# Attention heads in a two-layer trunk: order of the key tiles, place of the compressed branch, and which engine scales the probabilities

## The chip, the cores and the metric

The kernel runs on one core of a Trainium2 chip. The metric is device time in microseconds (us), the median of repeated executions; one further execution was taken with the hardware profiler, and its trace is what is read below. The core has five engines that run side by side and wait for each other by semaphores: TensorE (PE) for matmuls, VectorE (DVE), ScalarE (ACT) and GpSimd (POOL) for elementwise work, and SyncE (SP), which here issues DMAs. Matmuls write PSUM (eight banks of 128 x 512 f32); POOL works on SBUF tiles only in this kernel.

## What is computed

The reference is a decoder trunk of two layers on 512 tokens of width 1024. Each layer has one input projection, three mixers side by side (sparse attention with 8 heads, gated linear attention, spatial gating), an output projection, and a gated feed-forward part. The change lies in the attention mixer alone. Of its reference, cut to the parts that matter:

```python
p_cmp = masked_softmax(s, ...)                 # 31 compressed keys
o_cmp = einsum('bghqc,bcgd->bqghd', p_cmp, vc)
p = masked_softmax(s, tok <= t)                # selected blocks: with 512 tokens all of them
o_slc = einsum('bghqm,bgqmd->bqghd', p, vsel)
p = masked_softmax(s, wmask)                   # window of 512 tokens: all earlier ones
o_win = einsum('bghqk,bkgd->bqghd', p, vwb)
return gb[..., 0:1] * o_cmp + gb[..., 1:2] * o_slc + gb[..., 2:3] * o_win
```

So each head has two causal branches (br 0 selected, br 1 window) over 512 keys and one branch over 31 compressed keys, and its output is the gated sum of the three.

## The kernel before

The attention heads are computed one after the other in a Python loop over 8 heads (`hp`, `hh`) and two branches (`br`), written out into instructions; a scheduler of the framework then orders each engine's instructions ahead of time, so on each engine they run in one fixed order. Tokens are cut into four tiles of 128. For query tile i only the keys up to 128 (i + 1) matter, so its probabilities are a tile of 128 rows and 128, 256, 384 or 512 columns.

For one branch of one head the steps are:

- Scores. PE multiplies queries and keys into a PSUM bank (ring "s", three banks; lines L1217 and L1218 for tiles 0 and 1, both branches at once, L1236 and L1237 for tiles 2 and 3). DVE takes the row maxima (L1220, L1239), ACT the exponentials with their row sums (L1224, L1241).
- Scaling. DVE takes the reciprocals `rc` of the four row sums (L1246) and multiplies those of tiles 0 to 2 with the gate (`rr`, L1247). Then, in the order of `SORD`, DVE scales tiles 0 and 1 (L1255), ACT tile 2 (L1253) and POOL tile 3 (L1251), in place. POOL takes `rc` and the gate as two factors. A dependency written by hand lets POOL start only when DVE's second scaling is done.
- Turning. PE transposes the blocks of the scaled tiles into a PSUM bank (ring "t", two banks, L1264), in three groups `JG`: key tile 0 (4 blocks, 512 columns), key tile 1 (3 blocks, 384 columns), key tiles 2 and 3 (2 + 1 blocks, 384 columns).
- Eviction. Each group is cut into a high and a low part: ACT casts the bank to a tile PT (L301, inside the helper `split_psum`), DVE subtracts it from the bank (L302).
- Product. PE multiplies the values (`vst`) with the high and the low part (L1277, L1278) and adds up all of both branches in one PSUM bank, O (ring "o", one bank).

At the end of a head two more matmuls add the compressed branch (`pcT`, `vcb`; L1288, L1289), whose probabilities were made once per group of four heads. Then ACT copies one half of O (L1290), and DVE adds the other half to it (L1291), which frees O for the next head. After two heads the result is split in two parts by ACT (L301) and DVE (L302) for the output projection.

Matmuls of the output projection's other half (L338 to L340), for mixers that are already done, stand between the attention instructions on PE; their weights are cast by ACT (L320) and subtracted by DVE (L323). The query operands of later heads are copied by POOL (L1188).

Tiles are handed out from rings: the probabilities of tiles 0 and 1 have three buffers each and those of tiles 2 and 3 two (`P0B`), PT three.

## Time and profile before

| what | us |
|---|---|
| median of 3 runs | 1285.01 (1283.91 to 1285.46) |
| the profiled execution, its own time | 1285.18 |
| its span (first to last instruction) | 1283.4 |
| PE busy | 1257.9 (98%) |
| DVE busy | 916.0 (71%) |
| ACT busy | 676.1 (53%) |
| POOL busy | 152.9 (12%) |

The attention heads lie at about 180 to 280 us of the span (first layer) and 810 to 910 us (second layer). Busy time is the union of an engine's instructions as they are drawn; the ends of matmuls are modelled. A row of a group reads: line, engine, operation, output <- inputs, shapes, count | busy us, mean ns of one | idle us of the engine just before them, and what ended it. A row of the timeline reads: start, length, engine, line, operation, tiles, shapes, count, and in brackets the idle time before it and what ended it.

### The profile page before, as it was taken

Reading aid. Unit: us, or ns where it says so; the run is one execution under the profiler, and the core shown is the slowest. Engines: PE = TensorE matmul, PEld = TensorE weight load, DVE = VectorE, ACT = ScalarE, POOL = GpSimd, SP = SyncE. Lnnn points to the kernel's source line nnn. Section 1 sums busy time; section 2 is a strip of 40 time slices with the busy share of each in tenths; the row PEclk is TensorE's granted clock in tenths of the full one; section 3 lists DMA queues with packets and bytes.
Section 4 is the critical chain, followed back from the end, with each engine's and each line's share of the span. In section 5 each row is a group of like instructions: output and inputs, shape, how many; then the busy total and the mean of one; then the engine's idle time right before and its main releaser. Section 6 shows DMA issues by size and latency. Waiting matters only on the chain.

```text
span 1283.4 us, 18048 instructions
## 1 busy us (share of the span) xinstructions
PE 1257.9 (98%) x6678; PEld 1039.6 (81%) x6678; DVE 916.0 (71%) x1645; ACT 676.1 (53%) x1288; POOL 152.9 (12%) x157
## 2 busy tenths in 40 slices
PE   8999999999999999999999999999999999999997
PEld 7887788778888888888888887877788888888886
DVE  6667799977855775577546669998767457827775
ACT  5676357864533553354446743788544345515532
POOL 0101121112000100010301003111210001000102
PEclk9999999999999999999999999999999999999999
DMA  6461341034335885483335316210533448744811
GB/s 231 125 197 34 104 120 33 17 85 129 99 101 141 193 238 148 101 198 111 105 103 148 118 34 169 70 33 3 147 99 98 132 118 220 212 123 134 227 66 66
DMA packets 134203, 155.01 MB, mean 121 GB/s; under 512 B 9306, under 2 KB 86884, under 8 KB 134116
## 3 DMA queue, kind: packets, MB, share of 16 engines
q1 hardware_dynamic: 117392, 128.81, 33.1%
q0 software_dynamic: 10208, 20.84, 9.1%
q10 hardware_dynamic: 6516, 4.22, 1.4%
q8 instruction: 52, 0.85, 0.3%
q14 instruction: 35, 0.29, 0.1%
HBM read 149.92 MB, written 2.10 MB: 118 GB/s over the span
## 4 chain that ended last, share of the span: by engine, by line
PE 80%; DVE 10%; ACT 5%; DMA 2%; issue 2%; ACTq 0%; POOL 0%; DVEq 0%; POOLq 0%
PE banks L338 22%; PE banks L339 22%; PE banks L340 22%; PE banks L1264 2%; DVE PT L302 2%; PE banks L1277 1%; PE banks L1278 1%; DMA raw<-in_w_in_dram 1%; ACT hl L320 1%; PE banks L1601 1%; DVE nmx L1239 1%; PE banks L473 1%; DVE hl L323 1%; PE banks L971 1%; DVE w1h L745 1%
## 5 line engine op out<-in xcount | busy, mean ns | idle before, releaser
L320 ACT CAST hl<-raw 128x1024 fp32r<-128x1024 f32 (+3 forms) x170 | 175.2, 1034 | 226.0 <-PE banks L340 177.5
L323 DVE TENSOR_TENSOR hl<-raw,hl 128x1024 fp32r<-128x1024 f32 (+3 forms) x170 | 206.5, 1219 | 93.2 <-ACT hl L320 90.9
L338 PE MATMUL banks<-hl,kt 128*128 128x512 f32 (+2 forms) x688 | 258.0, 375 | 1.0 <-ACT hl L320 1.0
L339 PE MATMUL banks<-hl,kt 128*128 128x512 f32 (+2 forms) x688 | 256.4, 373 | 0.2 <-DVE hl L323 0.2
L340 PE MATMUL banks<-hl,kt 128*128 128x512 f32 (+2 forms) x688 | 256.2, 373 | 0.0
L339 PE MATMUL banks<-kt,hl 128*128 128x512 f32 x384 | 151.5, 394 | 0.1
L340 PE MATMUL banks<-kt,hl 128*128 128x512 f32 x384 | 151.1, 393 | 0.0
L338 PE MATMUL banks<-kt,hl 128*128 128x512 f32 x384 | 150.5, 394 | 0.0
L338 PEld LDWEIGHTS banks<-hl,kt 128*128 128x128 f32 x688 | 129.4, 188 | 23.4 <-ACT hl L320 1.8
L339 PEld LDWEIGHTS banks<-hl,kt 128*128 128x128 f32 x688 | 129.5, 188 | 22.0 <-DVE hl L323 0.6
L340 PEld LDWEIGHTS banks<-hl,kt 128*128 128x128 f32 x688 | 129.4, 188 | 21.9
L320 ACT CAST hl<-wx 128x1024 fp32r<-128x1024 f32 x48 | 50.5, 1052 | 79.8 <-PE banks L340 66.7
L339 PEld LDWEIGHTS banks<-kt,hl 128*128 128x128 f32 x384 | 72.2, 188 | 14.8 <-DVE kt L297 0.9
L340 PEld LDWEIGHTS banks<-kt,hl 128*128 128x128 f32 x384 | 72.1, 188 | 13.8
L338 PEld LDWEIGHTS banks<-kt,hl 128*128 128x128 f32 x384 | 72.0, 188 | 13.2 <-ACT kt L301 0.3
L323 DVE TENSOR_TENSOR hl<-wx,hl 128x1024 fp32r<-128x1024 f32 x48 | 58.7, 1223 | 19.0 <-ACT hl L320 18.8
L502 DVE TENSOR_TENSOR xT<-xT,banks 128x512 f32<-128x512 f32 x56 | 37.5, 680 | 48.0 <-PE banks L340 48.0
L339 PE MATMUL banks<-act,hl 128*128 128x512 f32 x172 | 67.0, 390 | 0.0
L340 PE MATMUL banks<-act,hl 128*128 128x512 f32 x172 | 66.9, 389 | 0.0
L338 PE MATMUL banks<-act,hl 128*128 128x512 f32 x172 | 66.9, 390 | 0.0
L302 DVE TENSOR_TENSOR PT<-banks,PT 128x384 fp32r<-128x384 f32 (+1 forms) x96 | 54.6, 597 | 13.3 <-ACT PT L301 12.4
L339 PE MATMUL banks<-hl,act 128*128 128x512 f32 (+1 forms) x164 | 63.0, 384 | 0.0
(356 smaller groups left out, 2394.5 us busy)
## 6 DMA issues: line engine op xcount, KB each, us to landing
raw<-in_w_gate_dram SPq DMA_DIRECT2D x44, 512.0 KB, 3.8
raw<-in_w_up_dram SPq DMA_DIRECT2D x44, 512.0 KB, 4.0
raw<-in_w_in_dram SPq DMA_DIRECT2D x32, 512.0 KB, 3.7
raw<-in_w_down_dram SPq DMA_DIRECT2D x36, 256.0 KB, 3.6
raw<-in_w_down_dram SPq DMA_DIRECT2D x18, 512.0 KB, 4.0
raw<-in_w_out_dram SPq DMA_DIRECT2D x16, 512.0 KB, 4.3
raw<-in_cmp_w_k_dram SPq DMA_DIRECT2D x8, 512.0 KB, 3.8
raw<-in_cmp_w_v_dram SPq DMA_DIRECT2D x8, 512.0 KB, 4.6
```

The source lines that it names most:

```text
L302: nc.vector.tensor_tensor(lo, src, hi.bitcast(F32), op=ALU.subtract)
L320: last_cast[:] = [nc.scalar.copy(hl[:, 0, 0:n], raw[:, 0:n])]
L323: e_.tensor_tensor(hl[:, 1, 0:n], raw[:, 0:n], hl[:, 0, 0:n].bitcast(F32), op=ALU.subtract)
L338: nc.tensor.matmul(ps, lh, rh, start=start, stop=False, skip_group_check=skip)
L339: nc.tensor.matmul(ps, lh, rl, start=False, stop=False, skip_group_check=skip)
L340: return nc.tensor.matmul(ps, ll, rh, start=False, stop=stop, skip_group_check=skip)
L473: ins = nc.tensor.matmul(pw[t], xkt[n][:, kk, p, t * P : t * P + P], eu[n][0][:, q, kk, :], start=n == 0 and p + q + kk == 0, stop=n == 3 ...
L502: nc.vector.tensor_tensor(xT[:, m, :], xT[:, m, :], ps, op=ALU.add)
L745: nc.vector.tensor_tensor(hl[:, 1], raw[:, q * 512 : q * 512 + 512], hl[:, 0].bitcast(F32), op=ALU.subtract)
L971: nc.tensor.matmul(banks[:, 2 + h, lv * 64 : lv * 64 + 64], Es[t][r, lv, :], xqs[t][r, lv, :], start=True, stop=True)
L1239: nc.vector.tensor_reduce(nmx, S[:, 0:n], axis=AX.X, op=ALU.max, negate=True)
L1264: nc.tensor.transpose(T[:, c : c + P], ps_[i][:, j * P : (j + 1) * P], ident)
```

## The change

Five things change in the attention heads:

- DVE no longer scales. POOL scales tile 3, then 1, then 0 (512, 256, 128 columns), each with `rc` and the gate as two factors; ACT still scales tile 2. The dependency between POOL and DVE is gone with DVE's scalings.
- `rr` is one column (tile 2) and not three.
- The order of scaling is 3, 2, 1, 0.
- The groups are turned and multiplied in the order key tiles (2, 3), then 1, then 0, in all branches but the first of head 0.
- In heads 1 to 7 the two matmuls of the compressed branch open the sum in O, and the product of key tile 0 of the second branch closes it. Head 0 is summed as before.

```diff
@@ -43,7 +43,7 @@
 WPOOL = {}
 WSITE = {}
 XKP = ()
-SORD = (0, 1, 2, 3)
+SORD = (3, 2, 1, 0)
 TT = "tttt"
 ATAGS = "gggggggg"
 OT = "o"
@@ -51,7 +51,7 @@
 PREP = {(0, 0): (("q", 0), ("q", 1)), (0, 1): (("c", 0),), (0, 3): (("d", 0),), (1, 0): (("q", 2),), (2, 0): (("q", 3),), (2, 3): (("c", 1),),
         (4, 0): (("d", 1),)}
 NBOTH = 2
-ISP = (3,)
+ISP = (3, 1, 0)
 ISA = (2,)
 PBK = {"g": 2, "s": 3, "t": 2, "o": 1}
 JG = ((0,), (1,), (2, 3))
@@ -1242,21 +1242,16 @@
                                 ps_.append(p_)
                             if br == 0:
                                 prep(h, 1)
-                            rc, rr = small(NT, "rc", 4), small(NT, "rr", 4)
+                            rc, rr = small(NT, "rc", 4), small(1, "rr", 4)
                             nc.vector.reciprocal(rc, den)
-                            nc.vector.tensor_tensor(rr[:, 0:3], rc[:, 0:3], gates[:, 0:3, 3 * h + 1 + br], op=ALU.mult)
-                            scaled = None
+                            nc.vector.tensor_tensor(rr, rc[:, 2:3], gates[:, 2:3, 3 * h + 1 + br], op=ALU.mult)
                             for i in SORD:
                                 if i in ISP:
-                                    p3 = nc.gpsimd.tensor_scalar(ps_[i], ps_[i], rc[:, i : i + 1], gates[:, i, 3 * h + 1 + br : 3 * h + 2 + br], op0=ALU.mult, op1=ALU.mult)
-                                elif i in ISA:
-                                    nc.scalar.activation(ps_[i], ps_[i], AF.Copy, scale=rr[:, i : i + 1])
+                                    nc.gpsimd.tensor_scalar(ps_[i], ps_[i], rc[:, i : i + 1], gates[:, i, 3 * h + 1 + br : 3 * h + 2 + br], op0=ALU.mult, op1=ALU.mult)
                                 else:
-                                    scaled = nc.vector.tensor_scalar(ps_[i], ps_[i], rr[:, i : i + 1], None, op0=ALU.mult)
-
-                            tc.add_manual_dep(p3.ins, scaled.ins.name, mybir.DependencyInfo(mybir.DependencyClass.Sync, mybir.DependencyReason.DATA),
-                                              reason="port")
-                            for js in JG:
+                                    nc.scalar.activation(ps_[i], ps_[i], AF.Copy, scale=rr)
+                            lhc = vcb[:, g, h4].rearrange("p s d -> p (s d)")
+                            for js in (JG if h == 0 and br == 0 else JG[::-1]):
                                 T = psum(TT[js[0]])
                                 c = 0
                                 for j in js:
@@ -1269,24 +1264,28 @@
                                 else:
                                     pf = mp.tile([P, c], F32, tag="PT", name=nm("PT"), bufs=3)
                                     nc.scalar.copy(pf, T[:, 0:c])
+                                if first and h > 0:
+                                    nc.tensor.matmul(O, lhc, pcT[g][0], start=True, stop=False)
+                                    nc.tensor.matmul(O, lhc, pcT[g][1], start=False, stop=False)
+                                    first = False
                                 c = 0
                                 for j in js:
                                     n = SEQ - j * P
                                     lhs = vst[:, j, br, g].rearrange("p s d -> p (s d)")
                                     if js[0] < JS:
                                         nc.tensor.matmul(O[:, j * P : SEQ], lhs, pt[:, 0, c : c + n], start=first, stop=False)
-                                        nc.tensor.matmul(O[:, j * P : SEQ], lhs, pt[:, 1, c : c + n], start=False, stop=False)
+                                        nc.tensor.matmul(O[:, j * P : SEQ], lhs, pt[:, 1, c : c + n], start=False, stop=h > 0 and br == 1 and j == 0)
                                     else:
                                         nc.tensor.matmul(O[:, j * P : SEQ], lhs.bitcast(F32), pf[:, c : c + n],
                                                          start=False, stop=False)
                                     first = False
                                     c += n
                         prep(h, 3)
-                        lhs = vcb[:, g, h4].rearrange("p s d -> p (s d)")
                         hs = slice(64 * hh, 64 * hh + 64)
                         ls = slice(64 - 64 * hh, 128 - 64 * hh)
-                        nc.tensor.matmul(O, lhs, pcT[g][0], start=False, stop=False)
-                        nc.tensor.matmul(O, lhs, pcT[g][1], start=False, stop=True)
+                        if h == 0:
+                            nc.tensor.matmul(O, lhc, pcT[g][0], start=False, stop=False)
+                            nc.tensor.matmul(O, lhc, pcT[g][1], start=False, stop=True)
                         nc.scalar.copy(oc[hs, :], O[ls, :])
                         nc.vector.tensor_tensor(oc[hs, :], oc[hs, :], O[hs, :], op=ALU.add)
                     split_psum(kt[:, hp % 2, 0, :], kt[:, hp % 2, 1, :], oc)
```

Line numbers behind the change are 5 lower at L1264 (L1259 after) and 1 lower at L1277 to L1291; POOL's scaling, L1251 before, is L1250.

How the instructions now stand is shown at three places around head 6 of the first layer. On PE, the first place is the step from head 5 to head 6. Before, the second matmul of head 5's compressed branch comes first, then the turns of head 6's first branch (`ident,P`), two score matmuls, and the first product of head 6:

```order
L1289 MATMUL banks<-pcT_2402,vcb_279 128x512
L1264 MATMUL banks<-ident,P_2649 128x128
L1264 MATMUL banks<-ident,P_2657 128x128
L1264 MATMUL banks<-ident,P_2665 128x128
L1264 MATMUL banks<-ident,P_2671 128x128
L1264 MATMUL banks<-ident,P_2657 128x128
L1264 MATMUL banks<-ident,P_2665 128x128
L1264 MATMUL banks<-ident,P_2671 128x128
L1236 MATMUL banks<-km_181_1599,qst_1807 128x384
L1237 MATMUL banks<-km_183_1601,qm_187_1605 128x384
L1277 MATMUL banks<-PT_2685,vst_277 128x512
```

In the changed kernel the same place on PE, from head 5's last product to head 6's first compressed matmul:

```order
L1277 MATMUL banks<-PT_2632,vst_277 128x512
L1259 MATMUL banks<-ident,P_2657 128x128
L1259 MATMUL banks<-ident,P_2665 128x128
L1259 MATMUL banks<-ident,P_2671 128x128
L1218 MATMUL banks<-km_183_1601,qm_187_1605 128x512
L1259 MATMUL banks<-ident,P_2649 128x128
L1259 MATMUL banks<-ident,P_2657 128x128
L1259 MATMUL banks<-ident,P_2665 128x128
L1259 MATMUL banks<-ident,P_2671 128x128
L1236 MATMUL banks<-km_181_1599,qst_1807 128x384
L1237 MATMUL banks<-km_183_1601,qm_187_1605 128x384
L1268 MATMUL banks<-pcT_2401,vcb_279 128x512
```

Between the last matmul of one head and the first of the next stand seven turns and two score matmuls before, and seven turns and three score matmuls now.

On DVE, the second place is the first branch of head 6, from its reciprocal on (`den` are the row sums, P_2649 and P_2657 tiles 0 and 1). Before:

```order
L1246 RECIPROCAL rc_2673<-den_2643 128x4
L1247 TENSOR_TENSOR rr_2674<-rc_2673,gates_280 128x3
L1239 TENSOR_REDUCE nmx_2716<-banks 128x1
L302 TENSOR_TENSOR PT_2620<-banks,PT_2620 128x384
L302 TENSOR_TENSOR PT_2628<-banks,PT_2628 128x384
L1255 TENSOR_SCALAR P_2649<-P_2649,rr_2674 128x128
L1255 TENSOR_SCALAR P_2657<-P_2657,rr_2674 128x256
```

In the changed kernel, DVE from the same reciprocal on, with the next branch's reciprocal (rc_2722), to the sum that frees O:

```order
L1246 RECIPROCAL rc_2673<-den_2643 128x4
L1220 TENSOR_REDUCE nmx_2763<-banks 128x2
L1247 TENSOR_TENSOR rr_2674<-rc_2673,gates_280 128x1
L302 TENSOR_TENSOR PT_2632<-banks,PT_2632 128x512
L302 TENSOR_TENSOR PT_2684<-banks,PT_2684 128x384
L1246 RECIPROCAL rc_2722<-den_2644 128x4
L1220 TENSOR_REDUCE nmx_2771<-banks 128x2
L1290 TENSOR_TENSOR tmp_2396<-tmp_2396,banks 64x512
```

The scalings are gone, and one row maximum now stands between the reciprocal and its product with the gate, which ACT's tile waits for.

On POOL, the third place is the queue of scalings around head 6. Before, from head 5's first branch to head 7's first:

```order
L1251 TENSOR_SCALAR P_2551<-P_2551,rc_2553,gates_280 128x512
L1251 TENSOR_SCALAR P_2598<-P_2598,rc_2600,gates_280 128x512
L1251 TENSOR_SCALAR P_2671<-P_2671,rc_2673,gates_280 128x512
L1251 TENSOR_SCALAR P_2718<-P_2718,rc_2720,gates_280 128x512
L1251 TENSOR_SCALAR P_2787<-P_2787,rc_2789,gates_280 128x512
```

In the changed kernel POOL's queue for head 5's second branch and head 6's first:

```order
L1250 TENSOR_SCALAR P_2600<-P_2600,rc_2602,gates_280 128x512
L1250 TENSOR_SCALAR P_2539<-P_2539,rc_2602,gates_280 128x256
L1250 TENSOR_SCALAR P_2531<-P_2531,rc_2602,gates_280 128x128
L1250 TENSOR_SCALAR P_2671<-P_2671,rc_2673,gates_280 128x512
L1250 TENSOR_SCALAR P_2657<-P_2657,rc_2673,gates_280 128x256
L1250 TENSOR_SCALAR P_2649<-P_2649,rc_2673,gates_280 128x128
```

Each branch has one scaling on POOL before and three now, the widest first.

## The prediction

> **What bounds the kernel now.** I read the page first.
>
> ```profile
> span 1283.4 us, 18048 instructions
> PE 1257.9 (98%) x6678; PEld 1039.6 (81%) x6678; DVE 916.0 (71%) x1645; ACT 676.1 (53%) x1288; POOL 152.9 (12%) x157
> ```
>
> TensorE (PE) is busy nearly all the time, and no engine is near it over the whole span. But an average hides stages, and the change touches one stage only, the attention heads, which run twice, once per layer. The view of busy time by windows shows these two stretches and, for comparison, a dense one (columns: stretch, its length, PE, PEld, DVE, ACT and POOL busy with their counts, clock, DMA).
>
> ```profile
> 180.00:280.00 100.00, 95.70 (x547) 76.15 (x546) 88.55 (x206) 77.88 (x214) 17.24 (x22) 1.00 0.17 42
> 810.00:910.00 100.00, 95.71 (x547) 76.30 (x546) 87.63 (x204) 77.19 (x212) 17.20 (x22) 1.00 0.17 44
> 330.00:340.00 10.00, 10.00 (x46) 8.29 (x45) 10.00 (x21) 5.76 (x11) 0.00 (x0) 1.00 0.24 60
> ```
>
> The two attention stretches are alike. PE idles 4.3 us in each, VectorE (DVE) is busy 88 us of 100, ScalarE (ACT) 78, and GpSimd (POOL) 17. So DVE is nearly full while POOL is nearly empty. PE's idle time here understates what PE loses, as two pieces of the timeline show.
>
> ```profile
> 329.77 0.39 PE L339 MATMUL banks<-kt,hl 128*128 128x512 f32 x1
> 330.00 0.39 PE L340 MATMUL banks<-kt,hl 128*128 128x512 f32 x1
> ...
> 235.76 0.28 PE L1218 MATMUL banks<-km,qm 128*128 128x256 f32 x1
> 236.36 0.44 PE L1277 MATMUL banks<-PT,vst 128*128 128x384 f32 x1 [0.32 <-ACT PT L301]
> ```
>
> In the dense stretch matmuls shown as 0.39 us long follow each other every 0.23 us: their drawn ends overlap the next start by 0.16 us. So the idle 0.32 us before the row at 236.36 is a stall of about 0.48 us, and stalls under 0.16 us are not drawn at all. What PE waits for stands in the view of waits over one attention stretch (waiting engine and line, releaser: us, times, longest).
>
> ```profile
> PEld banks L1277 <- ACT PT L301: 7.4, 18, 1.2
> PEld banks L1278 <- DVE PT L302: 3.9, 11, 0.9
> PE banks L1277 <- DVE tmp L1291: 1.5, 3, 0.8
> PEld banks L1264 <- POOL P L1251: 1.2, 4, 0.5
> PEld banks L1264 <- DVE P L1255: 0.4, 2, 0.2
> DVE PT L302 <- ACT PT L301: 6.2, 6, 1.5
> ACT P L1253 <- DVE rr L1247: 3.8, 4, 1.4
> ACT P L1241 <- DVE nmx L1239: 3.3, 4, 1.4
> ACT P L1241 <- PE banks L1264: 1.9, 2, 1.7
> ```
>
> The reader is to see three sources: the eviction of turned probabilities (ACT's cast L301, then DVE's subtraction L302), the accumulator O that the last head has not yet left (L1291), and scaled tiles that come late (POOL L1251, DVE L1255). DVE and POOL end 3.9 + 1.5 + 1.2 + 0.4 = 7.0 us of PE's waits per layer. That, not 98%, is what the change can touch.
>
> **The change part by part.** First, the scaling. These are the rows of what scales the four tiles of a branch (32 branches, 16 per layer).
>
> ```profile
> L1255 DVE TENSOR_SCALAR P<-P,rr 128x256 f32<-128x256 f32 x32 | 11.1, 346 | 0.1
> L1255 DVE TENSOR_SCALAR P<-P,rr 128x128 f32<-128x128 f32 x32 | 8.9, 278 | 0.2
> L1251 POOL TENSOR_SCALAR P<-P,rc,gates 128x512 f32<-128x512 f32 x32 | 24.6, 768 | 129.0 <-DVE P L1255 52.2 <-ACT P L1241 31.1 <-ACT P L1253 15.3
> L1253 ACT ACTIVATE P<-P,rr 128x384 f32<-128x384 f32 x32 | 20.0, 624 | 7.7 <-DVE rr L1247 7.7
> L1697 POOL MEMSET const-float32-1.0<- 128x1 f32 x1 | 0.1, 101 | 0.0
> 248.84 0.54 DVE L1255 TENSOR_SCALAR P<-P,rr 128x128 f32<-128x128 f32 x2
> ```
>
> DVE loses both L1255 of each branch. Their durations add to 0.62 us but overlap: the timeline gives the pair 0.54 us, so DVE loses 16 x 0.54 = 8.6 us per layer. POOL gains them. No row shows POOL scaling 256 or 128 columns. From below, in proportion to 512 columns, they cost 0.38 and 0.19 us; from above, if width did not matter, 0.77 each. A POOL instruction of one column took 0.10 us, so I take 0.10 us plus 1.3 ns a column: 0.43 and 0.27 us. POOL then works 0.77 + 0.43 + 0.27 = 1.47 us a branch (1.34 to 2.30), 11 us more per layer on an engine busy 17 of 100 us; as load that is free. ACT's part is unchanged.
>
> As latency it is shorter than before. At the branch shown in the order, DVE stood before at: reciprocal, product, a 512-wide maximum, two 384-wide subtractions, two scalings, and only then POOL.
>
> ```profile
> L1246 DVE RECIPROCAL rc<-den 128x4 f32<-128x4 f32 x32 | 5.5, 172 | 2.3 <-ACT P L1241 1.8
> L1247 DVE TENSOR_TENSOR rr<-rc,gates 128x3 f32<-128x3 f32 x32 | 6.6, 206 | 0.3
> L1239 DVE TENSOR_REDUCE nmx<-banks 128x1 f32<-128x512 f32 x32 | 21.7, 679 | 0.0
> L302 DVE TENSOR_TENSOR PT<-banks,PT 128x384 fp32r<-128x384 f32 x64 | 34.3, 551 | 11.8 <-ACT PT L301 11.3
> L1220 DVE TENSOR_REDUCE nmx<-banks 128x2 f32<-128x256 f32 x16 | 6.7, 416 | 0.5 <-PE banks L1218 0.5
> ```
>
> From the end of the reciprocal that was 0.21 + 0.68 + 2 x 0.55 + 0.54 + 0.77 = 3.3 us until all four tiles were ready. Now POOL starts at the reciprocal and is through after 1.47 us, and ACT's tile follows a 256-wide maximum and the product: 0.42 + 0.21 + 0.62 = 1.25 us. So all tiles are there some 1.8 us sooner, and I count the waits for scaled tiles, 1.2 + 0.4 = 1.6 us per layer, as gone.
>
> The removed dependency kept POOL off DVE's scalings, which are gone too. But DVE's product rr remains, and the timeline shows what happens when it meets POOL.
>
> ```profile
> 247.86 0.15 DVE L1247 TENSOR_TENSOR rr<-rc,gates 128x3 f32<-128x3 f32 x1
> 249.38 0.66 DVE L1220 TENSOR_REDUCE nmx<-banks 128x2 f32<-128x512 f32 x1
> 249.57 0.77 POOL L1251 TENSOR_SCALAR P<-P,rc,gates 128x512 f32<-128x512 f32 x1 [5.75 <-ACT P L1253]
> 249.96 0.39 DVE L1247 TENSOR_TENSOR rr<-rc,gates 128x3 f32<-128x3 f32 x1
> ```
>
> Alone it takes 0.15 us; started during POOL's scaling it ended only when POOL did, 0.39 us later (249.96 + 0.39 = 250.35, POOL 249.57 + 0.77 = 250.34). Now POOL starts right after the reciprocal, and rr mostly stands one maximum (0.42 to 0.68 us) behind it, so it begins in the last 0.1 to 0.35 us of POOL's first tile: I charge 0.2 us a branch, 16 x 0.2 = 3.2 us per layer (from 0, when rr directly follows the reciprocal, to 0.9, when it waits out all three tiles: about 1.47 - 0.55). Before, such meetings cost the mean 206 against 150, 0.056 x 16 = 0.9 us. DVE's load goes from 88.6 to 88.6 - 8.6 + 3.2 - 0.9 = 82.3 us per layer. The Trainium skill, page "SBUF — State Buffer", section "SBUF: two separate sides", calls the shared pair of ports an exclusive lock that a DVE operation with two SBUF inputs and a POOL operation hold in turn; rr has two such inputs, and the rows above agree.
>
> Second, the order of the groups. Tiles 2 and 3 are ready first and are now turned first, and the widest product (key tile 0) is last. Each group still needs PE turn, ACT cast, DVE subtraction, PE. With 6.3 us of DVE freed, the subtraction waits less in DVE's queue; but in 6 cases DVE itself idled for ACT's cast (6.2 us), which freed DVE time does not mend. Of the 11 waits for L302 I take 5 as queueing: 3.9 x 5/11 = 1.8 us.
>
> Third, the compressed branch leads. Its operand is ready long before, so nothing new is waited for; it only takes the wait for O in place of the first PV product. That wait is ACT's copy and DVE's sum.
>
> ```profile
> L1290 ACT COPY tmp<-banks 64x512 f32<-64x512 f32 x16 | 9.3, 580 | 6.7 <-PE banks L1289 6.5
> L1291 DVE TENSOR_TENSOR tmp<-tmp,banks 64x512 f32<-64x512 f32 x16 | 10.9, 684 | 6.5 <-ACT tmp L1290 6.1
> ```
>
> 0.58 + 0.68 = 1.26 us must pass. In the order shown, PE has seven turns and two 384-wide score products in between before, and the same plus one 512-wide score product (0.23 us) after; and DVE no longer has L1255 in front of the sum. I count half of the 1.5 us: 0.8. Instruction counts on PE and ACT do not change, nor does a DMA or SP's queue; on POOL's queue the copies L1188 can now stand behind up to 1.47 us of scaling, but they feed a later head, and the weight loads L1467 that POOL issues behind the last scaling start 0.43 + 0.27 us later at most, for data that only the feed-forward part, behind the whole output projection, uses.
>
> Sum per layer: 1.6 + 1.8 + 0.8 = 4.2 us. Two layers: 8.4. The profiled execution took 1285.18 us, so 1276.8; the median of 1285.01 is 0.17 lower, so **1276.6 us**, with 1272 to 1281 when the halves go either way. About 0.2%, 2.6 us, is what a measurement of this kernel can tell from no change.
>
> **The rivals.** *More than that (0.16).* If DVE is the true bound of the stage, all of the 8.6 us per layer comes off: ACT also idles 3.8 + 3.3 us for DVE's rr and maxima, and sooner maxima mean sooner casts. 1285.0 - 17.3 = 1267.7. Against it: rr is now delayed by POOL.
>
> *POOL and DVE lock each other out (0.12).* If rr waits out not one tile but more, 0.54 us a branch, DVE has back all that it lost: 1285. At the upper bound of 0.9 DVE is 6 us per layer worse off; below 0.2 it is my forecast. The Trainium skill, page "Perfetto Trace Analysis", section "Optimizing Scalar/DVE Operations", says that moving work between these two engines may not help as they share a port; this rival is what that would mean here. For it: the rows of L1247. Against it: the maximum at 249.38 ran into the same POOL instruction and still took 0.66 us; it reads PSUM, as the maxima and evictions do, and these are most of DVE's work here.
>
> *ACT takes over (0.11).* The largest wait, 7.4 us per layer, is for ACT's cast, and ACT's instructions stay. If only the tiles' lateness goes and the rest moves to ACT, 0.8 us per layer remains: 1283.5. This is the case in which the change does nothing that it seems to do.
>
> *Slower: exponentials wait for tiles 0 and 1 (0.15).* These tiles have three buffers, and a head takes two. Before, tile 0 was turned by the first group and was free; now it is last. ACT already waits for turns to free tiles (L1241 after L1264, 1.9 us in 2 cases). ACT works in order, so casts queue behind a waiting exponential. At 0.9 us, as in those two cases, at each of the 14 steps from head to head, it is 12.6 us, and with my gain of 8.4 gives 1285 + 4.2 = 1289. It decides from 0.6 us a step (8.4 / 14).
>
> **How the numbers follow.** Forecast 0.46, the rivals 0.16, 0.12, 0.11 and 0.15. Faster by over 0.2% (below 1282.4): 0.45 of the forecast, all 0.16, 0.03 of the lock and 0.05 of ACT, together 0.69. Slower (above 1287.6): 0.13 and 0.03 of the lock, 0.16. The same: 0.15. Range 1267 to 1287: it takes in the larger gain and the lock, and leaves out most of the slower case and what lies below the larger gain.
>
> **What would show it.** Right: in both stretches DVE falls by some 6 us of work, no row of DVE scaling, POOL's two new rows near 430 and 270 ns, rr's mean about 0.35 us, the waits of PE for L302, L1291 and POOL down by about 4 us per layer, and the attention stretch 4 us shorter in each layer with all else unmoved. Wrong: rr at 0.6 us or more (the lock); ACT waiting for turns at the exponentials of tiles 0 and 1 by over 0.6 us a head; or the same stretch length with the wait for ACT's cast grown by what the others lost.

## The result, and the profile after

The changed kernel takes 1291.89 us (median of 4 runs, 1291.04 to 1292.68) against 1285.24 (4 runs, 1283.91 to 1285.55) for the kernel before, measured beside it: a ratio of 1.0054, 95% interval 1.0042 to 1.0067. It is slower by 6.65 us, where 8.4 us of gain were forecast. The profiled run of the changed kernel has a span of 1289.8 us, 6.4 more than before. Of all executions below, one of the five of f4 ran at a granted clock of 0.601 and took 2016.7 us; it is left out.

Its page, first part, and its busy time by windows over the two attention stretches:

```profile
span 1289.8 us, 18051 instructions
PE 1259.7 (98%) x6678; PEld 1037.8 (80%) x6678; DVE 908.3 (70%) x1581; ACT 677.1 (53%) x1288; POOL 188.1 (15%) x221
```

```profile
180.00:280.00 100.00, 93.43 (x530) 72.68 (x529) 83.06 (x173) 77.81 (x213) 35.16 (x54) 1.00 0.11 33
810.00:910.00 100.00, 93.09 (x524) 72.20 (x523) 84.86 (x173) 78.82 (x216) 33.55 (x54) 1.00 0.11 33
```

DVE got lighter about as forecast (88.55 to 83.06 us of 100 in the first layer, 87.63 to 84.86 in the second; 82.3 was forecast) and POOL took the work over. But PE, the engine that sets the end, did fewer matmuls in the same 100 us (530 instead of 547) and idled 6.6 us instead of 4.3. What it waited for, from the view of waits over one attention stretch of the changed kernel (line numbers differ from those before: turns are L1259, products L1276 and L1277, the compressed products L1268 and L1269, the sum of O L1290; in the runs further down turns are one of L1258 to L1265, POOL's scaling is L1250 or L1251):

```profile
PEld banks L1276 <- ACT PT L301: 4.4, 17, 0.4
PEld banks L1259 <- POOL P L1250: 4.1, 6, 1.0
PEld banks L1268 <- DVE tmp L1290: 2.8, 6, 1.0
PEld banks L1259 <- ACT P L1252: 2.5, 6, 0.8
PEld banks L1277 <- DVE PT L302: 2.3, 7, 0.8
PE banks L1259 <- POOL P L1250: 2.0, 4, 0.6
PEld banks L1217 <- ACT P L1241: 1.7, 4, 0.6
PE banks L1268 <- DVE tmp L1290: 1.4, 3, 0.7
PE banks L1259 <- ACT P L1252: 0.8, 2, 0.6
DVE nmx L1239 <- PE banks L1237: 3.5, 5, 1.4
ACT P L1252 <- DVE rr L1247: 6.0, 7, 1.3
```

The waits for turned and evicted probabilities (L301, L302) shrank from 7.4 and 3.9 us. The waits for scaled tiles, which were 1.2 for POOL's (and 0.3 in the row of PE itself) and 0.4 for DVE's, are now 4.1 + 2.0 for POOL's and 2.5 + 0.8 for ACT's. The groups by form of the changed kernel say why POOL's and ACT's tiles are late:

```profile
L1250 POOL TENSOR_SCALAR P<-P,rc,gates 128x512 f32<-128x512 f32 x32 | 24.8, 775 | 109.8 <-DVE rc L1246 95.2 <-PE banks L1237 7.9 <-PE banks L1122 3.5
L1250 POOL TENSOR_SCALAR P<-P,rc,gates 128x256 f32<-128x256 f32 x32 | 20.6, 645 | 0.0
L1250 POOL TENSOR_SCALAR P<-P,rc,gates 128x128 f32<-128x128 f32 x32 | 16.6, 517 | 0.0
L1252 ACT ACTIVATE P<-P,rr 128x384 f32<-128x384 f32 x32 | 19.8, 620 | 12.5 <-DVE rr L1247 12.5
L1247 DVE TENSOR_TENSOR rr<-rc,gates 128x1 f32<-128x1 f32 x32 | 11.2, 349 | 0.1
```

POOL's three scalings add to 0.775 + 0.645 + 0.517 = 1.94 us, not 1.47. These are means. The medians are 0.772, 0.558 and 0.451; six of the 64 small scalings took 0.99 to 1.54 us, each of them beside a DVE subtraction that reads two SBUF tiles (L323 four times, L302 of `kt` twice). None of PE's stalls counted below stands behind one of these six. The product rr takes 349 ns on the mean instead of 206, and ACT idles 12.5 us for it ahead of tile 2 over the kernel instead of 7.7.

Drawn idle time counts PE's weight loads too, which run under the matmul before. A fairer count is worked out from the start times in the trace: each matmul's start minus the start of the one before it, less the pitch that matmuls of its width have in dense stretches (0.227 us for 512 columns, 0.172 for 384, 0.118 for 256, 0.109 for 128); what is over by 0.12 us or more is a stall, put down to what released it. A stall on a score bank is a score product that waits until an exponential has read the bank it is to write. Both layers together, in us, for the two kernels and four of the experiments below:

| | before | after | e3 | e6 | e11 | e12 |
|---|---|---|---|---|---|---|
| scaled tiles (POOL, ACT, DVE) | 2.1 | 9.5 | 5.0 | 3.5 | 2.6 | 9.5 |
| of these behind POOL's | 1.7 | 5.9 | 4.5 | 2.2 | 2.2 | 8.9 |
| of these behind ACT's | 0 | 3.6 | 0.5 | 1.4 | 0.4 | 0 |
| evictions (L301, L302) | 10.5 | 5.5 | 7.9 | 7.9 | 6.1 | 6.9 |
| O not yet free | 4.1 | 4.2 | 3.2 | 3.5 | 1.6 | 1.3 |
| score banks (exponentials late) | 0.5 | 3.5 | 2.9 | 2.5 | 0.2 | 1.3 |
| all such stalls | 18.0 | 24.2 | 20.3 | 17.5 | 12.4 | 20.3 |
| span | 1283.4 | 1289.8 | 1285.3 | 1282.4 | 1276.7 | 1284.2 |
| PE work from a branch's last score product to its first turn, mean | 6.66 | 5.61 | 5.38 | 5.85 | 6.55 | 5.56 |
| branches (of 32) whose first turn is of tile 1 | 0 | 10 | 8 | 4 | 2 | 0 |

The stalls grow by 6.2 us, the span by 6.4. Scaled tiles alone bring 7.4, late score banks 3.0; evictions give back 5.0. The last two rows are read from the order of PE's instructions, the first of them in the pitches above. They show what I had not looked at: where the turns stand. One place in the changed kernel, first PE's order and then the timeline:

```
L1236 MATMUL banks<-km_181_1599,qst_1807 128x512
L1259 MATMUL banks<-ident,P_2539 128x128
L1237 MATMUL banks<-km_183_1601,qm_186_1604 128x512
L1236 MATMUL banks<-km_181_1599,qst_1807 128x384
L1237 MATMUL banks<-km_183_1601,qm_186_1604 128x384
```

```profile
256.44 0.16 DVE L1246 RECIPROCAL rc<-den 128x4 f32<-128x4 f32 x1
256.80 1.74 POOL L1250 TENSOR_SCALAR P<-P,rc,gates 128x512 f32<-128x512 f32 x3 [4.51 <-DVE rc L1246]
256.97 0.60 DVE L1247 TENSOR_TENSOR rr<-rc,gates 128x1 f32<-128x1 f32 x1
257.34 0.39 PE L1236 MATMUL banks<-km,qst 128*128 128x512 f32 x1
258.17 0.33 PE L1259 MATMUL banks<-ident,P 128*128 128x128 f32 x1 [0.44 <-POOL P L1250]
258.25 0.48 PE L1237 MATMUL banks<-km,qm 128*128 128x512 f32 x1
258.83 0.69 DVE L1239 TENSOR_REDUCE nmx<-banks 128x1 f32<-128x512 f32 x1 [1.26 <-PE banks L1237]
```

P_2539 is tile 1. The scheduler put its turn ahead of all other turns of its branch and between the two products of one score of the next branch. POOL, which takes tile 3 first, delivers tile 1 second (its row at 256.80 is all three), at 258.11. PE starts nothing between 257.34 and 258.17, and the score product behind the turn waits with it; so does DVE's maximum (idle 1.26 us), and the next exponentials after that. rr began 0.17 us after POOL did and ended with POOL's first scaling, 0.60 us instead of 0.15.

### The profile page after: what moved, and what is told of

The parts are those of the page before. It is cut to its first block, busy times and chain, and to the rows that moved or that the text cites. A ratio compares the mean times of both kernels' runs of the same rounds, so it can differ in the third digit from the quotient of the medians.

```text
span 1289.8 us, 18051 instructions
## 1 busy us (share of the span) xinstructions
PE 1259.7 (98%) x6678; PEld 1037.8 (80%) x6678; DVE 908.3 (70%) x1581; ACT 677.1 (53%) x1288; POOL 188.1 (15%) x221
## 4 chain that ended last, share of the span: by engine, by line
PE 79%; DVE 8%; ACT 7%; issue 3%; DMA 2%; POOL 1%; ACTq 0%; DVEq 0%; POOLq 0%
PE banks L338 22%; PE banks L339 22%; PE banks L340 22%; PE banks L1259 1%; ACT hl L320 1%; DVE PT L302 1%; DMA raw<-in_w_in_dram 1%; DVE hl L323 1%; PE banks L1276 1%; PE banks L473 1%; PE banks L1600 1%; PE banks L971 1%; PE banks L1277 1%; POOL P L1250 1%; ACT PT L301 1%
## 5 line engine op out<-in xcount | busy, mean ns | idle before, releaser
L323 DVE TENSOR_TENSOR hl<-raw,hl 128x1024 fp32r<-128x1024 f32 (+3 forms) x170 | 206.5, 1218 | 97.8 <-ACT hl L320 96.0
L1250 POOL TENSOR_SCALAR P<-P,rc,gates 128x512 f32<-128x512 f32 (+2 forms) x96 | 60.8, 646 | 109.8 <-DVE rc L1246 95.2
L323 DVE TENSOR_TENSOR hl<-wx,hl 128x1024 fp32r<-128x1024 f32 x48 | 58.7, 1224 | 18.1 <-ACT hl L320 18.0
L302 DVE TENSOR_TENSOR PT<-banks,PT 128x384 fp32r<-128x384 f32 (+1 forms) x96 | 54.8, 597 | 20.9 <-ACT PT L301 20.5
```

What stands on the lines that cost most here:

```text
L302: nc.vector.tensor_tensor(lo, src, hi.bitcast(F32), op=ALU.subtract)
L323: e_.tensor_tensor(hl[:, 1, 0:n], raw[:, 0:n], hl[:, 0, 0:n].bitcast(F32), op=ALU.subtract)
L1250: nc.gpsimd.tensor_scalar(ps_[i], ps_[i], rc[:, i : i + 1], gates[:, i, 3 * h + 1 + br : 3 * h + 2 + br], op0=ALU.mult, op1=ALU.mult)
```

## The experiments

Three theories stood against each other. **Turns too early:** the scaled tiles come at a time that PE's fixed order does not allow for; then moving only the turns in PE's order mends it. **Lock:** DVE's rr and POOL's scalings hold each other up; then an rr that POOL doesn't hold up mends it. **Order:** the reversed groups and the leading compressed product are themselves dear; then the order alone shows the loss and the scaling alone doesn't. Each ratio is against the kernel before, run on the same chip beside it; where versions are compared in us, it is by what each takes more or less than that kernel beside it (the changed kernel +6.65).

**e1_order, e2_pool, e3_rr_one_input, e4_unscaled: each half alone, the lock, and POOL's small scalings.** e1 is the changed kernel with the scaling as before:

```diff
-SORD = (3, 2, 1, 0)
-ISP = (3, 1, 0)
+SORD = (0, 1, 2, 3)
+ISP = (3,)
 (and lines 1245 to 1258 of the kernel before in place of the new scaling)
```

> Order alone: key tiles 2 and 3 first and the compressed branch leading, as in the changed kernel, but scaling as before (DVE tiles 0 and 1, ACT 2, POOL 3 behind DVE). LATE (the loss is POOL's: its small scalings and the wait for them at the turns, which grew by about 7.5 us per layer, while the waits for evictions fell by 5.4): faster than before by 2 to 6 us, 1279 to 1283. ORDER (the loss is in the new order: the wait for O grew from 1.5 to 4.2 us per layer, and the scheduler places turns too early): slower than before, 1288 to 1292.

Measured 1295.97 us, ratio 1.0091 (1.0077 to 1.0104), slower than either theory had it. PE's waits in one layer:

```profile
PEld banks L1265 <- POOL P L1251: 5.5, 11, 1.4
PE banks L1265 <- POOL P L1251: 2.5, 6, 1.2
PEld banks L1265 <- ACT P L1253: 1.9, 5, 0.7
```

The order alone is dearer than the whole change, with the same kind of wait: POOL's tile 3 is ready last, behind DVE's two, and belongs to the group that is now turned first. e2 is the kernel before with the new scaling only; its edit against the changed kernel:

```diff
-                            for js in (JG if h == 0 and br == 0 else JG[::-1]):
+                            for js in JG:
 (and the compressed product behind the head again, as before)
```

> POOL alone: POOL scales tiles 3, 1, 0 and rr is one column, but groups in the old order and the compressed branch last. LATE: all three tiles are needed by the very first group of turns, so slower than before by at least what the changed kernel lost, 1291 to 1300. ORDER: DVE is relieved and nothing else changes, 1278 to 1286.

Measured 1288.29, ratio 1.0032 (1.0019 to 1.0044), between the two ranges.

```profile
PEld banks L1258 <- POOL P L1250: 5.3, 8, 1.3
PE banks L1258 <- POOL P L1250: 2.7, 5, 0.9
```

The scaling alone costs 4.0 us, with POOL's waits again; now tiles 0 and 1 are ready last and turned first. Neither half is harmless, and they don't add: 11.7 + 4.0 is 15.7, together they cost 6.65. e3 is the changed kernel with rr computed from one tensor and one scalar operand:

```diff
-nc.vector.tensor_tensor(rr, rc[:, 2:3], gates[:, 2:3, 3 * h + 1 + br], op=ALU.mult)
+nc.vector.tensor_scalar(rr, rc[:, 2:3], gates[:, 2, 3 * h + 1 + br : 3 * h + 2 + br], None, op0=ALU.mult)
```

> The changed kernel with rr = rc times gate made by an operation that reads one tensor and takes the gate as a scalar operand, where before it read two SBUF tensors. LOCK (rr waits for POOL's scaling of tile 3, mean 349 ns against 150, and tile 2 with it): rr falls to 150 to 160 ns everywhere and the time to 1283 to 1287. LATE: rr falls too, but POOL's tiles stay late, 1289 to 1292.

Measured 1287.08, ratio 1.0025 (1.0015 to 1.0034). Its groups by form:

```profile
L1247 DVE TENSOR_SCALAR rr<-rc,gates 128x1 f32<-128x1 f32 x32 | 6.6, 207 | 0.3
L1252 ACT ACTIVATE P<-P,rr 128x384 f32<-128x384 f32 x32 | 19.8, 619 | 5.1 <-DVE rr L1247 5.1
L1250 POOL TENSOR_SCALAR P<-P,rc,gates 128x256 f32<-128x256 f32 x32 | 17.9, 559 | 0.0
L1250 POOL TENSOR_SCALAR P<-P,rc,gates 128x128 f32<-128x128 f32 x32 | 14.5, 453 | 0.0
```

It takes 2.8 us more than the kernel before, 3.8 less than the changed kernel. rr's own time shrank by 11.2 - 6.6 = 4.6 us on DVE, which isn't full (to 207 ns on the mean, where 150 to 160 was expected); ACT's idle time for rr, which is on the way to PE, fell by 12.5 - 5.1 = 7.4 us, and PE's stalls behind ACT's tile from 3.6 to 0.5 us. That 3.1 us fits the lock. The rest is not shown to be its doing: the scheduler wrote another order for this form of rr, with 8 first turns of tile 1 and not 10. POOL's small scalings take 0.56 and 0.45 us, with no long one among them. What is left of the loss, e3 doesn't mend. e4 is the changed kernel without any scaling of tiles 0 and 1:

```diff
 for i in SORD:
+    if i < 2:
+        continue
```

> The changed kernel with the scaling of tiles 0 and 1 left out altogether (their rows are neither divided by the row sum nor gated), so POOL scales tile 3 alone and the two late tiles cost nothing. LATE: the gain that the order and the relief of DVE should bring shows, 1277 to 1283. ORDER: still slower than before, 1288 or more. LOCK: rr still meets POOL's tile 3, so between, 1285 to 1288.

Measured 1281.08, ratio 0.9978 (0.9969 to 0.9987). With POOL left with one tile, no wait of PE for POOL remains, and the rest of the change gains 0.2%. So what is lost hangs on when POOL's tiles are ready.

**e5_dve_back, e6_turn_later, e7_later_one_input, e8_before_later: who scales, and where the turns stand.** e5 is the changed kernel in which DVE scales tiles 1 and 0 again (rr of three columns, no hand-written dependency):

```diff
-ISP = (3, 1, 0)
+ISP = (3,)
...
+                                    nc.vector.tensor_scalar(ps_[i], ps_[i], rr[:, i : i + 1], None, op0=ALU.mult)
```

> The changed kernel (new order of groups, compressed branch leading, scaling in the order 3, 2, 1, 0) with DVE scaling tiles 1 and 0 again, from a three-column rr, and no dependency between POOL and DVE. It gives the new order a scaling that suits it, which the run with the old scaling order did not. LATE (the turns wait for POOL's scaled tiles): the small tiles take 0.35 and 0.28 us on DVE and not 0.56 and 0.45 on POOL, waits for scaled tiles fall from 9.5 us in both layers to under 5 and the time to 1283 to 1288. LOCK: DVE's scalings now meet POOL's tile 3 and wait for it as rr does, DVE loses up to 0.77 us a branch, 1292 to 1300. ORDER: 1290 or more, with the waits for O and evictions as in the changed kernel.

Measured 1288.09, ratio 1.0031 (1.0020 to 1.0041): with the new order, DVE's scalings are cheaper than POOL's by 6.65 - 3.78 = 2.9 us, yet not as cheap as before the change. e6 is the changed kernel with one thing altered in the program, the scheduler's priority of the turns, set back by 20 steps; engines and instructions are the same, though other instructions shift in the order too:

```diff
+with tc.high_priority(offset=-20):
     for j in js:
         for i in range(j, NT):
             nc.tensor.transpose(T[:, c : c + P], ps_[i][:, j * P : (j + 1) * P], ident)
```

> The changed kernel with every turn given a lower priority in the scheduler (20 steps), so that it places more PE work between a branch's last score and its first turn: mean 6.16 us against 5.61, smallest 3.09 against 2.84. No instruction changes its engine or its cost. PLACE (the scheduler puts turns before POOL and ACT can be done; the fixed order on PE is what turns late tiles into lost time): waits for scaled tiles fall by half and the time to 1283 to 1287. LATE without PLACE (POOL is short of time as such): the waits only move to the products behind, 1290 to 1293.

Measured 1283.65, ratio 0.9997 (0.9988 to 1.0005).

```profile
PEld banks L1260 <- POOL P L1250: 1.6, 2, 0.8
PE banks L1260 <- POOL P L1250: 0.7, 2, 0.4
PEld banks L1260 <- ACT P L1252: 1.2, 3, 0.7
PE banks L1260 <- ACT P L1252: 0.3, 1, 0.3
```

The whole loss is gone, with the lock mostly in place (ACT still idles 10.7 us for rr over the kernel, where it idled 12.5), and the waits for scaled tiles fell from 4.1 + 2.0 + 2.5 + 0.8 = 9.4 to 1.6 + 0.7 + 1.2 + 0.3 = 3.8 us a layer in these rows. The stalls on scaled tiles fell by 6.0 of the 7.3 us. PE work ahead of the first turn is 5.85 us in the kernel that ran, not the 6.16 of the expectation, so the mean grew by little; the branches that turn tile 1 first fell from 10 to 4. e7 is e6 with the rr of e3:

```diff
+with tc.high_priority(offset=-20):
+nc.vector.tensor_scalar(rr, rc[:, 2:3], gates[:, 2, 3 * h + 1 + br : 3 * h + 2 + br], None, op0=ALU.mult)
```

> Both: turns at the lower priority and rr made by an operation with one tensor input. LOCK and PLACE add: 1279 to 1284, at or under the kernel before. If they mend the same wait, no better than either alone: 1283 to 1287.

Measured 1280.64, ratio 0.9974 (0.9965 to 0.9983), 3.0 us less than e6. e8 is the control, the kernel before with its turns set back by 20:

```diff
+with tc.high_priority(offset=-20):   (in the kernel before)
```

> Control: the kernel before with the same lower priority of the turns. Its scaled tiles are waited for only 2.1 us in both layers, so PLACE has nothing to mend: within 0.3% of before, 1281 to 1289. If any reshuffling of the order moves the time by 0.5%, this shows it, and the other comparisons mean less.

Measured 1285.46, ratio 1.0007 (0.9998 to 1.0016). At this offset later turns by themselves gain nothing; they repair what the new scaling broke.

**e9_old_order, e10_later40, e11_later80, e12_before_sooner: is the order needed, how far back, and the same fault made in the kernel before.** e9 is e2 with the rr of e3 and turns set back by 20, so e7 with the old order of groups; against e7:

```diff
-for js in (JG if h == 0 and br == 0 else JG[::-1]):
+for js in JG:
 (and the compressed product behind the head again, as before)
```

> POOL scales tiles 3, 1, 0, rr with one tensor input and turns at the lower priority, but groups in the old order and the compressed branch last: the run at 1280.6 without its new order. If the new order is worth something once the tiles are in time, this is slower: 1284 to 1288, since the first group needs all four tiles and POOL's third scaling is what it waits for. If only DVE's relief counts, 1279 to 1282.

Measured 1290.98, ratio 1.0054 (1.0040 to 1.0068), 3 us above the expected range.

```profile
PEld banks L1259 <- POOL P L1250: 6.2, 9, 1.4
PE banks L1259 <- POOL P L1250: 3.9, 6, 1.2
```

With tile 0 turned first, POOL is too late at this priority as it was in e2: of the orders tried, only the reversed one goes with POOL's scaling. e10 and e11 are e7 with other offsets:

```diff
-with tc.high_priority(offset=-20):
+with tc.high_priority(offset=-40):   (e10)
+with tc.high_priority(offset=-80):   (e11)
```

> The run at 1280.6 with turns 40 steps later in priority and not 20: the smallest PE work between last score and first turn is 3.86 us and not 3.09, the mean 5.61 and not 5.68. PLACE, if the closest branches are what counts: 1277 to 1281. If the mean counts: 1280 to 1283.

> The same with 80 steps: mean 6.55 us, smallest 2.95. PLACE by the mean: waits for scaled tiles nearly gone, 1277 to 1281. Rival: turns that come later hold the tiles' buffers longer, so exponentials and with them scores wait (ACT P L1241 ahead of PE), and the time rises again, 1282 to 1288.

Measured 1281.29, ratio 0.9982 (0.9973 to 0.9991), and 1279.92, ratio 0.9971 (0.9960 to 0.9981). e11 is the fastest version found and beats both kernels. Its attention stretch by windows, and its waits for scaled tiles in one layer:

```profile
180.00:280.00 100.00, 97.52 (x558) 77.89 (x558) 81.76 (x173) 77.86 (x211) 34.37 (x54) 1.00 0.18 48
```

```profile
PEld banks L1260 <- POOL P L1250: 1.6, 3, 0.8
PE banks L1260 <- POOL P L1250: 0.7, 2, 0.4
PEld banks L1260 <- ACT P L1252: 0.7, 2, 0.3
```

PE does 558 matmuls in the stretch, against 547 before and 530 in the changed kernel. The mean PE work ahead of the first turn is not all that decides: e10 has 5.61 us, as the changed kernel has, with 4 first turns of tile 1 and not 10, and gains. e12 is the kernel before, its turns brought forward:

```diff
+with tc.high_priority(offset=80):   (in the kernel before)
```

> The kernel before with turns 80 steps sooner in priority: PE work from last score to first turn falls from a mean of 6.66 us to 5.56, about what the changed kernel had (5.61), with DVE scaling and all else as before. PLACE: scaled tiles come late here too, waits for them rise from 2.1 us to 5 or more in both layers, time 1287 to 1293. If POOL's small scalings alone make the loss: no change, 1283 to 1287.

Measured 1286.89, ratio 1.0022 (1.0013 to 1.0031).

```profile
PEld banks L1265 <- POOL P L1251: 5.4, 11, 0.8
PE banks L1265 <- POOL P L1251: 2.4, 8, 0.4
```

The stall of the changed kernel can be made in the kernel before by the turns' place alone: 9.5 us of stalls on scaled tiles, as in the changed kernel, while evictions and O cost less there, so that the time grew by only 0.2% and lies within the range expected for no change. The stalls, not the time, show that the turns' place sets this wait without POOL's new work.

**f1_later80_two_inputs, f2_dve_back_later80, f3_later240, f4_before_later80: what e11 needs.** f1 is e11 with the two-input rr of the change:

```diff
-nc.vector.tensor_scalar(rr, rc[:, 2:3], gates[:, 2, 3 * h + 1 + br : 3 * h + 2 + br], None, op0=ALU.mult)
+nc.vector.tensor_tensor(rr, rc[:, 2:3], gates[:, 2:3, 3 * h + 1 + br], op=ALU.mult)
```

> The changed kernel with turns 80 steps later, rr still with two SBUF inputs: the run at 1279.9 with the old rr. LOCK counts where tiles are in time: 1282 to 1285. LOCK is covered by the later turns: 1279 to 1281.

Measured 1284.88, ratio 1.0005 (0.9996 to 1.0014): 4.5 us worse than e11 (+0.52 against -3.95), with a mean rr of only 264 ns:

```profile
L1247 DVE TENSOR_TENSOR rr<-rc,gates 128x1 f32<-128x1 f32 x32 | 8.4, 264 | 0.3
L1252 ACT ACTIVATE P<-P,rr 128x384 f32<-128x384 f32 x32 | 19.9, 622 | 5.2 <-DVE rr L1247 5.2
```

ACT's tile in e11:

```profile
L1252 ACT ACTIVATE P<-P,rr 128x384 f32<-128x384 f32 x32 | 19.8, 620 | 8.4 <-DVE rr L1247 8.3
```

In f1 ACT idles less for rr than in e11, and no stall of PE stands behind ACT's tile. What grew are stalls on score banks, 6.7 us against 0.2, in an order that differs as well. So the one-input rr is worth 3.0 to 4.5 us in three pairs of versions (the changed kernel and e3, e6 and e7, f1 and e11), but only in e3 do the stalls show the path.

f2 is e5 with its turns set back by 80:

```diff
+with tc.high_priority(offset=-80):   (in e5)
```

> The new order with DVE scaling tiles 1 and 0 again (rr of three columns, two inputs) and turns 80 steps later. If what the change gains is DVE's 8.6 us per layer, this is slower than the same with POOL scaling (the run beside it): 1284 to 1290. If only the place of the turns counts: 1279 to 1283.

Measured 1287.96, ratio 1.0027 (1.0018 to 1.0037). Without POOL's relief of DVE the new order gains nothing at either place of the turns. f3 sets e7's turns back by 240:

```diff
-with tc.high_priority(offset=-20):
+with tc.high_priority(offset=-240):
```

> rr with one input and turns 240 steps later: mean PE work from last score to first turn 7.26 us, where 80 steps gave 6.55. PLACE: as good as 80 or better, 1277 to 1280. Rival: buffers held longer make exponentials wait, 1282 or more.

Measured 1303.37, ratio 1.0146 (1.0133 to 1.0160). Now the chain behind the turns starves, in one layer:

```profile
DVE PT L302 <- ACT PT L301: 19.9, 18, 3.7
ACT PT L301 <- PE banks L1260: 15.1, 13, 3.6
```

ACT waits 15.1 us for turns. In the kernel before it was 7.5:

```profile
ACT PT L301 <- PE banks L1264: 7.5, 7, 1.8
```

f4, the control for e11, is the kernel before with its turns set back by 80:

```diff
+with tc.high_priority(offset=-80):   (in the kernel before)
```

> Control: the kernel before with turns 80 steps later (mean 7.16 us against 6.66). If the 4 us that the best run is ahead come from the change's parts once they are placed, this stays at 1283 to 1287; if they come from later turns alone, it is at 1279 to 1282 too.

Measured 1297.7 (four executions), ratio 1.0101 (1.0087 to 1.0115), slower than either range. The order alone can move this kernel by 1%, so the bare time of a version with another order proves little; what carries e6 and e12 is that the stalls on scaled tiles moved with it.

## Why the prediction was wrong, point by point

**DVE's relief: about right.** 82.3 us a layer forecast, 83.06 and 84.86 measured, in stretches in which PE did fewer matmuls; over the whole span DVE's busy time fell by 916.0 - 908.3 = 7.7 us, where 2 x 6.3 = 12.6 was forecast. No DVE scaling is left.

**rr against POOL: right in size, wrong in what it costs.** I charged 0.2 us a branch and a mean of 0.35 us; it was 349 ns. I put that on DVE's load only. It lies on the path to ACT's tile 2: with the one-input form (e3) 3.1 us of stalls behind that tile and 3.8 us of time went. The lock rival asked for 0.54 us a branch before it decided; the mean rr grew by 0.14, and it cost time all the same. As the Trainium skill has it on page "Perfetto Trace Analysis", section "Optimizing Scalar/DVE Operations", moving work between these two engines might not help because of the port. The change as made did not help (ratio 1.0054), in part for that reason, as e3 shows; with a rr of one tensor input and turns that stand later the same move helps (ratio 0.9971).

**POOL's small scalings: under-sized.** 0.43 and 0.27 us taken from a one-column row and the 512-wide one; 0.56 and 0.45 in e3, which are also the changed kernel's medians. The chain was 1.94 us on the mean, within the bounds of 1.34 to 2.30.

**The step that failed: "So all tiles are there some 1.8 us sooner, and I count the waits for scaled tiles, 1.2 + 0.4 = 1.6 us per layer, as gone."** They grew to 9.4 us a layer. The tiles did come sooner, but by 0.96 us: from the end of the reciprocal to the end of the last of the four scalings, the mean of all 32 branches was 3.33 us before (3.3 was counted, from one branch) and 2.37 now (1.47 was counted; ACT's tile 2 takes 2.08 and not 1.25). And I counted to the last tile, while PE stops first at the tile that it turns first. That one was there after 1.85 us before (tile 0 in all branches) and after 1.86 now (tile 2 in 22 branches, tile 1 in 10): no sooner. I also took the turns as standing where they had stood. But the scheduler writes PE's order anew: the turns moved nearer to the scores (6.66 to 5.61 us of PE work on the mean), and in 10 of 32 branches the first turn is of tile 1, POOL's second. That was to be seen in the order, without any run. e6 shows the turns' place as the cause: only their priority was set anew, the stalls on scaled tiles fell from 9.5 to 3.5 us, and 7.3 us came back (+6.65 to -0.66). e12 makes the same stall in the kernel before.

**Evictions: right for L302, and larger in all.** 1.8 us a layer forecast for L302, whose row fell from 3.9 to 2.3; ACT's cast L301 fell too, from 7.4 to 4.4, which was not forecast. The stalls on both fell by 5.0 us over two layers. How much of it only moved to the turns, which PE now waits for first, was not separated.

**The compressed branch ahead: no gain.** 0.8 us a layer forecast; stalls for O were 4.1 us and are 4.2.

**Not forecast at all:** stalls on score banks, 0.5 to 3.5 us, from exponentials that come late. The timeline shows one way: a waiting turn holds back the score products behind it.

**The slower rival named the wrong mechanism.** Exponentials waiting for turns to free tiles 0 and 1 (1.9 us a layer before) no longer stand among the changed kernel's waits of 0.2 us or more. That mechanism's kind of loss, turns that come too late for what hangs on them, appeared in f3.

**What stays open.** Every edit makes the scheduler write a new order, so the parts don't add up to the whole. The offsets 20, 40 and 80 give 1280.6, 1281.3 and 1279.9 us, within about a thousandth, so no best offset is claimed between them. How much of the gain of e3, e7 and e11 is the lock's and how much their orders' was not separated either. How much of e1's loss is the order and how much its scaling order, which fits it badly, was not separated. Why f4 loses 1% stays open, and so does what sets the stalls on score banks, which are 6.7 us in f1.

## What to carry to other kernels

When a scheduler fixes each engine's order ahead of time, a cheaper step is not a sooner one: compare when an operand is ready with where its first reader stands in the other engine's order, before and after, and count how often the first reader is of the operand that is ready late. Work moved to an idle engine lengthens a chain if that engine is slower per piece, and its readers then have to stand later; move them, and try both directions on the kernel before as a control. A tiny instruction at the head of a chain deserves the form that isn't held up, even if that form is a little longer alone (0.20 us and not 0.15 here).

## What the runs showed of the hardware

**A one-column DVE product can take four times its time.** In the changed kernel 24 of the 32 two-input products began during a POOL scaling and took 0.38 us on the mean, up to 0.62, where one takes 0.15 alone; with a scalar operand (e3), 22 began so, and all 32 took 0.20 to 0.22 us. It holds the other way round too: the six long scalings of POOL in the changed kernel (0.99 to 1.54 us, against medians of 0.56 and 0.45) all met a DVE subtraction of two SBUF tiles. The Trainium skill, page "SBUF — State Buffer", section "Who interferes with whom", says that of DVE's operations those with two SBUF inputs contend with a POOL operation that reads SBUF, and those in a 2-port mode with any; the trace agrees on the first. On the second it may: this 16-column operation of the changed kernel has one tensor input, and it took 0.16 us before:

```profile
229.06 1.74 POOL L1250 TENSOR_SCALAR P<-P,rc,gates 128x512 f32<-128x512 f32 x3 [1.21 <-DVE rc L1246]
229.25 0.62 DVE L1157 TENSOR_SCALAR cd<-cd 128x16 f32<-128x16 f32 x1
```

It ended at 229.87, within 0.04 us of POOL's first scaling (229.06 + 0.78). Which mode it ran in, no row shows.

**POOL has a large fixed cost per instruction.** 512 columns took 0.768 us (kernel before), 256 and 128 columns 0.559 and 0.453 (e3). That is about 0.35 us and 0.82 ns a column, so cutting POOL's work into narrow tiles saves little: a quarter of the width costs 59% of the time.
